# A batched matmul whose last store sends each partition's fourth row in 14 short transfers

## The chip, the cores and the metric

The kernel runs on one core of a Trainium2 chip. The metric is the device time of one execution in microseconds (us). Before the change it is 511.72 us, the median of 3 runs (511.66 to 512.26). A core has five engines that run side by side, PE (matmul), DVE (vector), ACT (scalar), POOL (GpSimd) and SP (which here only waits and issues transfers), and 16 transfer engines ("DMA engines" in the profile) that move data between the chip's main memory and the core's 128-partition memory.

## The reference

```python
def setup_inputs():
    batch, m, k, n = 32, 512, 1024, 768
    return {
        "x": np.random.randn(batch, m, k).astype(np.float32),
        "weight": np.random.randn(batch, k, n).astype(np.float32),
    }

def reference(x, weight):
    return np.matmul(x, weight).astype(np.float32)
```

32 independent products of a 512 x 1024 matrix with a 1024 x 768 matrix, all in float32 at the kernel's edges. The inputs are 64 MiB of x and 96 MiB of weight, the output is 48 MiB.

## The kernel before

The 32 batches are worked in 16 pairs. POOL loads x and weight and turns them into bfloat16 on the way (`load_x`, `load_w`); a pair of batches comes in one transfer of each, except at the edges of the program. PE transposes x (L173), DVE copies the transposed blocks out of PE's accumulator memory (L219, for the last pair L227), and PE multiplies (L165 and L138). ACT and DVE copy the results to `outs`, a buffer of four slots of one pair each (L261, L265, L270, L272).

Outputs of pairs 0 to 13 leave in one transfer for each pair, which POOL issues (`store`, L119). Pair 14 leaves in one transfer as well, issued by SP. The two batches of the last pair, 30 and 31, leave separately, each as soon as its own copies are done: `store_one` (L121 to L123), issued by SP. For these two, a partition holds four consecutive rows of the output, 4 x 768 float32 values, so that the store of one batch is 128 partitions x 3,072 values, 12,288 B of consecutive memory for each partition. `last_out(b)` is the place of batch b in `outs`, `one_view[b]` the place in the output.

SP's program (`on_sp`) first hands on the arrival of loads to PE in the order of the batches, then issues the three stores in a row: pair 14 (L379), batch 30 (L380), batch 31 (L381). Each of them waits for its own copies (`copied`), and counts its landing on the semaphore `s_fin`, 16 for a transfer. After that SP releases `s_zero` (L382), which POOL needs before it clears the semaphores. POOL's last step (`clear_on_pool`) is to wait until `s_fin` has reached 48, that is, until all three stores have landed (L392); after this the program ends.

Of the kernel before, what the change touches and what calls it, by code (L numbers as in the profile page):

```python
# [12 lines left out]
def kernel(  # L13
# [7 lines left out]
    B, M, K = x.shape  # L21
    _, _, N = weight.shape
# [5 lines left out]
    N2 = 2 * N  # L28
    ROW = MT * N
    PAIRS = B // 2  # L30
    HELD = 2
    GROUPS = 2 * MT
    W_SLOTS, X_SLOTS, OUT_SLOTS = 4, 2, 4

    pe, dve, act, pool, sp = nc.tensor, nc.vector, nc.scalar, nc.gpsimd, nc.sync
# [4 lines left out]
    one_view = out.rearrange("b (mi mo) n -> b mi (mo n)", mi=P)  # L40
# [20 lines left out]
    def sem(name):  # L61
        sems.append(nc.alloc_semaphore(name))
        return sems[-1]
# [7 lines left out]
    s_a, s_ap, s_d, s_dp = sem("s_a"), sem("s_ap"), sem("s_d"), sem("s_dp")  # L71
    s_st = [sem(f"s_st{i}") for i in range(OUT_SLOTS)]
    s_fin = sem("s_fin")


    def mm_done(b):
# [6 lines left out]
    def last_out(b):  # L83

        return outs[(PAIRS - 1) % OUT_SLOTS][:, ROW * (b % 2):ROW * (b % 2 + 1)]

# [3 lines left out]
    def together(b):  # L90
        return W_SLOTS <= b < B - 2

    def load_w(b):
        if together(b):
            if b % 2 == 0:
                pool.wait_ge(s_mm, mm_done(b + 1 - W_SLOTS))
                slots = all_ws[:, b // 2 % 2].rearrange("p r ko n -> p r (ko n)")
                pool.dma_start(out=slots, in_=w_two_view[b // 2]).then_inc(s_w[b % W_SLOTS], 16)  # L98
            return
        if b >= W_SLOTS:  # L100
            pool.wait_ge(s_mm, mm_done(b - W_SLOTS))
        pool.dma_start(out=ws[b % W_SLOTS], in_=w_view[b]).then_inc(s_w[b % W_SLOTS], 16)  # L102

    def loads_of_w(b):

        return sum(not (together(i) and i % 2) for i in range(b % W_SLOTS, b + 1, W_SLOTS))

    def load_x(k):
        if k >= X_SLOTS:
            pool.wait_ge(s_mm, mm_begun(k - X_SLOTS))  # L110
        pool.dma_start(out=xs[k % X_SLOTS], in_=x_view[k]).then_inc(s_x[k % X_SLOTS], 16)  # L111

    def copied(eng, j):
        eng.wait_ge(s_ap, j + 1)
        eng.wait_ge(s_dp, j + 1)

    def store(eng, a, sem):
        copied(eng, 4 * a + 3)
        eng.dma_start(out=two_view[a], in_=outs[a % OUT_SLOTS]).then_inc(sem, 16)  # L119

    def store_one(b):  # L121
        copied(sp, 2 * b + 1)
        sp.dma_start(out=one_view[b], in_=last_out(b)).then_inc(s_fin, 16)  # L123

# [49 lines left out]
    def take(s):  # L176
        pe.wait_ge(s, 1).then_inc(s, -1)  # L177
# [13 lines left out]
    def on_pe():  # L191
# [4 lines left out]
        pe.wait_ge(s_ident, 1)  # L196
        with nc.Fori(0, PAIRS, engines=[mybir.EngineType.PE], hint_back_edge=True):
            take(s_xr)
# [75 lines left out]
    def cast_first(eng, copy, rows):  # L274

        for mo in rows:
            if mo == MT - 1:
                eng.wait_ge(s_cast, 1)
                eng.wait_ge(s_rest, 16)
            last = copy(xs[0][:, mo], x_first[:, mo])  # L280
        return last

    def on_dve():
# [6 lines left out]
        cast_first(dve, dve.tensor_copy, range(MT // 2)).then_inc(s_cast, 1)  # L290
        turns = PAIRS // OUT_SLOTS

# [42 lines left out]
    def landed(eng, slot, n, ready, uses=1):  # L335

        eng.wait_ge(slot, 16 * n).then_inc(ready, uses)

    def on_pool():
# [17 lines left out]
        def stores(first, last):  # L357
            for a in range(max(first, 0), last):
                store(pool, a, s_st[a % OUT_SLOTS])


        for k in range(PAIRS - 2):
            load_x(k + 2)
# [3 lines left out]
            load_w(2 * k + 5)  # L367
        stores(PAIRS - 3 - HELD, PAIRS - 2)

    def on_sp():  # L370
        for b in range(B):
            if b == 0:
                sp.wait_ge(s_cast, 2).then_inc(s_xr, 1)
            elif b % 2 == 0:
                k = b // 2
                landed(sp, s_x[k % X_SLOTS], (k + 1) // X_SLOTS, s_xr)
            if not (together(b) and b % 2):
                landed(sp, s_w[b % W_SLOTS], loads_of_w(b), s_wr, 1 + together(b))
        store(sp, PAIRS - 2, s_fin)  # L379
        store_one(B - 2)  # L380
        store_one(B - 1)  # L381
        sp.sem_inc(s_zero, 1)  # L382

    def clear_on_pool():

        for i, s in enumerate(s_st):
            pool.wait_ge(s, 16 * len(range(i, PAIRS - 2, OUT_SLOTS)))
        pool.wait_ge(s_zero, 2)
        used = range(sems[0].num, s_fin.num)
        pool.dma_reset(used)  # L390
        pool.sem_clear(used)
        pool.wait_ge(s_fin, 48).then_inc(s_fin, -48)  # L392

    sp.dma_start(x_first, x_view[0, :, :MT])
    with tc.tile_critical(sync_engine=mybir.EngineType.Activation, no_gpsimd_drain=True):  # L395
        on_pool()
        tc.wait_critical_data_deps()
        on_pe()
        on_dve()
        on_act()  # L400
        on_sp()
        clear_on_pool()
# [30 lines left out]
```

## Time and profile before

| what | value |
|---|---|
| median of 3 runs | 511.72 us (511.66 to 512.26) |
| the profiled execution: span from first to last instruction | 509.6 us |
| bytes read from main memory, written | 167.77 MB, 50.33 MB |
| mean rate over the span | 428 GB/s |
| PE busy | 429.4 us, 84% |
| DVE, ACT, POOL busy | 211.7, 114.1 and 29.6 us |
| last store issued by SP | 498.43 us |
| from its issue to its landing | 10.2 us |

The profile comes from one execution of its own, whose span is 509.6 us; the runs' times cover a little more than the span. Lines such as "L123" are lines of the kernel. "SPq" is SP's issuing of transfers. In the rows of windows the columns are: the stretch in us from the span's start, its length, the busy time of PE, PE's weight loads, DVE, ACT and POOL (with the number of instructions), the clock granted to PE, the mean busy share of the 16 transfer engines, and the GB/s that they moved. A packet's bytes are put down to the window in which the packet starts, so in short windows a share can be above 1. In rows of transfers the last number is the us from the issue to the landing; in rows of one line's instructions the three numbers are the shortest, the median and the longest duration in ns, then the first and the last start in us.

### The profile page before, as it was taken

The numbers are of one execution on the slowest core, as the hardware profiler recorded it, in microseconds if no ns is written. First come the engines' busy times: TensorE is split into PE (matmuls) and PEld (weight loads), VectorE is DVE, ScalarE is ACT, GpSimd is POOL, SyncE is SP. The second block draws the span as 40 slices with busy tenths as digits, with TensorE's granted clock in tenths as the row PEclk, the third lists the DMA queues.
The fourth block names the chain that finished last, engine by engine and source line by source line (L and its number), as shares of the span: only waits on it lengthen the run. The fifth ranks groups of instructions, "written<-read, shape, count | busy, mean of one in ns | idle before, by whom it ended". The sixth has DMA issues, their size and how long they took to land. (4 is left out here: it accounts for less than half of the span.)

```text
span 509.6 us, 5832 instructions
## 1 busy us (share of the span) xinstructions
PE 429.4 (84%) x2560; PEld 172.8 (34%) x1536; DVE 211.7 (42%) x330; ACT 114.1 (22%) x195; POOL 29.6 (6%) x55
## 2 busy tenths in 40 slices
PE   0899989999899399993999949999399994999990
PEld 0525342443325034250343513434034341433420
DVE  1436362454635136351373514635146351454631
ACT  1131312223130231302313023230231302223230
POOL 3000000000101001010010100100001000100000
PEclk9999998999999799996999979999699997999996
DMA  8999999999999999999999999999999999999998
GB/s 262 216 211 216 225 207 221 215 305 247 221 212 230 432 234 214 217 237 432 226 215 217 247 433 216 218 217 259 420 217 217 219 267 408 218 215 229 432 430 347
DMA packets 9299, 135.29 MB, mean 266 GB/s; under 512 B 848, under 2 KB 848, under 8 KB 848
## 3 DMA queue, kind: packets, MB, share of 16 engines
q0 software_dynamic: 8720, 126.88, 96.8%
q1 hardware_dynamic: 576, 8.39, 4.0%
q14 instruction: 3, 0.02, 0.0%
HBM read 167.77 MB, written 50.33 MB: 428 GB/s over the span
## 5 line engine op out<-in xcount | busy, mean ns | idle before, releaser
L165 PE MATMUL pm<-w,xT 128*128 x1024 | 346.2, 389 | 42.0 <-DVE outs L270 38.7
L138 PE MATMUL pm<-w,xT 128*128 x1024 | 284.7, 278 | 0.0
L165 PEld LDWEIGHTS pm<-w,xT 128*128 128x128 bf16 x1024 | 102.3, 100 | 282.8 <-issue 241.0
L270 DVE COPY outs<-pm 64x512 f32<-64x512 f32 x128 | 88.2, 689 | 207.7 <-DVEq L268 206.3
L261 ACT COPY outs<-pm 64x512 f32<-64x512 f32 x128 | 74.2, 580 | 272.6 <-PE pm L138 168.4
L173 PE MATMUL pt<-ident,x 128*128 128x128 f32 x512 | 84.5, 307 | 24.8 <-PEq L177 14.5
L219 DVE COPY xT<-pt 128x1024 bf16<-128x1024 bf16 x120 | 77.7, 687 | 63.9 <-PE pt L173 63.6
L173 PEld LDWEIGHTS pt<-ident,x 128*128 128x128 f32 x512 | 71.2, 210 | 40.0 <-DVE xT L219 18.8
L265 ACT COPY outs<-pm 64x512 f32<-64x512 f32 x64 | 37.0, 579 | 99.5 <-PE pm L138 99.3
L272 DVE COPY outs<-pm 64x512 f32<-64x512 f32 x64 | 43.9, 686 | 0.0
L98 POOL DMA_DIRECT2D w<-in_weight_dram x13 | 9.2, 708 | 264.6 <-PE pm L138 264.6
L111 POOL DMA_DIRECT2D x<-in_x_dram x15 | 8.4, 557 | 123.2 <-PE pm L138 92.4
L119 POOL DMA_DIRECT2D out_dram<-outs x14 | 7.5, 539 | 7.1 <-DVE outs L272 7.1
L227 DVE COPY xT<-pt 128x512 bf16<-128x512 bf16 x16 | 5.7, 418 | 4.1 <-PE pt L173 4.1
L280 DVE CAST x<-outs 128x1024 bf16<-128x1024 f32 x2 | 1.3, 692 | 11.0 <-DMA outs<-in_x_dram 11.0
L102 POOL DMA_DIRECT2D w<-in_weight_dram x6 | 3.2, 544 | 26.5 <-PE pm L138 26.3
L280 ACT ACT_TABLE_LOAD x1 | 1.3, 1283 | 10.7 <-DMA outs<-in_x_dram 10.7
L280 ACT CAST x<-outs 128x1024 bf16<-128x1024 f32 x2 | 2.0, 1042 | 0.0
L340 POOL DMA_DIRECT2D x<-in_x_dram x1 | 0.7, 670 | 0.8 <-POOLq L417 0.8
L344 POOL TENSOR_SCALAR_AFFINE_SELECT ident<-ident 128x128 f32<-128x128 f32 x1 | 0.3, 284 | 0.2 <-POOL ident L342 0.2
L342 POOL MEMSET ident<- 128x128 f32 x1 | 0.2, 232 | 0.0
L417 POOL MEMSET const-float32-0.0<- 128x1 f32 x1 | 0.1, 99 | 0.2 <-issue 0.2
(3 smaller groups left out, 0.3 us busy)
## 6 DMA issues: line engine op xcount, KB each, us to landing
out_dram<-outs POOLq DMA_DIRECT2D x14, 3072.0 KB, 40.1
w<-in_weight_dram POOLq DMA_DIRECT2D x13, 3072.0 KB, 32.9
x<-in_x_dram POOLq DMA_DIRECT2D x15, 2048.0 KB, 34.3
w<-in_weight_dram POOLq DMA_DIRECT2D x6, 1536.0 KB, 30.5
out_dram<-outs SPq DMA_DIRECT2D x1, 3072.0 KB, 18.7
out_dram<-outs SPq DMA_DIRECT2D x2, 1536.0 KB, 13.6
outs<-in_x_dram SPq DMA_DIRECT2D x1, 2048.0 KB, 9.7
x<-in_x_dram POOLq DMA_DIRECT2D x1, 1024.0 KB, 11.6
```

What stands on the lines that cost most here:

```text
L98: pool.dma_start(out=slots, in_=w_two_view[b // 2]).then_inc(s_w[b % W_SLOTS], 16)
L111: pool.dma_start(out=xs[k % X_SLOTS], in_=x_view[k]).then_inc(s_x[k % X_SLOTS], 16)
L119: eng.dma_start(out=two_view[a], in_=outs[a % OUT_SLOTS]).then_inc(sem, 16)
L138: return pe.add_instruction(mybir.InstMatmult(name=nc.get_next_instruction_name(), engine=mybir.EngineType.PE, ins=[pe.lower_ap(moving), p ...
L165: last = pe.matmul(*args, start=(ko == 0), stop=(ko == KT - 1))
L173: last = pe.transpose(pts[g % 2][:, j, :], words[:, mo, j::JT], ident)
L219: return dve.tensor_copy(both[g // 2][:, :, :, g % 2].rearrange("p b j i r -> p j b i r"), pt)
L227: last = dve.tensor_copy(rows, pt[:, :, b])
L261: last = act.copy(*piece)
L265: act.copy(*pieces(b, p, 2)[0]).then_inc(s_ap, 1)
L270: last = dve.tensor_copy(*piece)
L272: dve.tensor_copy(*pieces(b, p, 2)[1]).then_inc(s_dp, 1)
```

## The change

Batch 30's store stays as it is. Batch 31's store is cut by columns: the first three of the four rows of each partition (2,304 values, 9,216 B) leave in one transfer over all 128 partitions, and the fourth row (768 values, 3,072 B) in 14 transfers over 15, 14, 13, 12, 11, 11, 10, 9, 8, 7, 6, 5, 4 and 3 partitions, which add up to 128. The 14 count on a semaphore of their own, `s_tail`, and POOL waits for it ahead of its last wait.

```diff
+    TAIL = (15, 14, 13, 12, 11, 11, 10, 9, 8, 7, 6, 5, 4, 3)
...
+    s_tail = sem("s_tail")
...
     def store_one(b):
         copied(sp, 2 * b + 1)
-        sp.dma_start(out=one_view[b], in_=last_out(b)).then_inc(s_fin, 16)
+        if b < B - 1:
+            sp.dma_start(out=one_view[b], in_=last_out(b)).then_inc(s_fin, 16)
+            return
+        most, at = ROW - N, 0
+        sp.dma_start(out=one_view[b, :, :most], in_=last_out(b)[:, :most]).then_inc(s_fin, 16)
+        for n in TAIL:
+            part = slice(at, at + n)
+            row = last_out(b)[part, most:]
+            sp.dma_start(out=one_view[b, part, most:], in_=row).then_inc(s_tail, 16)
+            at += n
...
         pool.dma_reset(used)
         pool.sem_clear(used)
+        ends = 16 * len(TAIL)
+        pool.wait_ge(s_tail, ends).then_inc(s_tail, -ends)
         pool.wait_ge(s_fin, 48).then_inc(s_fin, -48)
```

Only SP's program and the end of POOL's differ. SP's before, from the first load on (L394 the load, L119 the store of pair 14, L123 those of batches 30 and 31):

```order
L394 DMA outs<-in_x_dram 128x4096
L428 UNCONDITIONAL_BRANCH
L119 DMA out_dram<-outs 128x6144
L123 DMA out_dram<-outs 128x3072 x2
L395 UNCONDITIONAL_BRANCH
```

And SP's now, from the larger part of batch 31 on (L129), with the first rows of the 14 short transfers (L133):

```order
L129 DMA out_dram<-outs 128x2304
L133 DMA out_dram<-outs 15x768
L133 DMA out_dram<-outs 14x768
L133 DMA out_dram<-outs 13x768
L133 DMA out_dram<-outs 12x768
L133 DMA out_dram<-outs 11x768 x2
L133 DMA out_dram<-outs 10x768
L133 DMA out_dram<-outs 9x768
```

Where one issue stood for batch 31, 15 stand now, one after another on SP, with no wait between them.

## The prediction

> **What bounds the kernel now.** I read the page first (share of the transfer engines, the chain that ended last), then the windows of the last 12 us, then the rows of the store's own line.
>
> ```profile
> DMA  8999999999999999999999999999999999999998
> q1 hardware_dynamic: 576, 8.39, 4.0%
> 496.28 0.08 issue
> 496.36 0.68 DVE outs L270
> 497.04 0.71 DVEq L395
> 497.75 0.61 DVE outs L272
> 498.43 0.33 SPq L123 DMA_DIRECT2D out_dram<-outs  x1
> 498.50:506.50 8.00, 0.00 (x0) 0.00 (x0) 0.00 (x0) 0.00 (x0) 0.00 (x0) 0.58 1.00 429
> ```
>
> The transfer engines are at 0.9 or more in 38 of 40 slices, so transfers set the pace of the whole program. The chain of waits stops at the last copy on DVE, which ends at 498.36 us; 0.07 us later SP issues the last store. From there on no engine computes (every column of 498.50:506.50 is zero) and only stores move, at 429 GB/s. The span ends at 509.6, so the last 11.2 us are transfers and a closing. The change acts there alone.
>
> ```profile
> 505.94:506.40 0.46, 0.00 (x0) 0.00 (x0) 0.00 (x0) 0.00 (x0) 0.00 (x0) 0.50 1.00 427
> 506.40:506.80 0.40, 0.00 (x0) 0.00 (x0) 0.00 (x0) 0.00 (x0) 0.00 (x0) 0.50 1.15 492
> 506.80:507.30 0.50, 0.00 (x0) 0.00 (x0) 0.00 (x0) 0.00 (x0) 0.00 (x0) 0.50 0.58 246
> 507.30:507.70 0.40, 0.00 (x0) 0.00 (x0) 0.00 (x0) 0.00 (x0) 0.00 (x0) 0.50 0.30 123
> 507.70:508.10 0.40, 0.00 (x0) 0.00 (x0) 0.00 (x0) 0.00 (x0) 0.00 (x0) 0.50 0.08 31
> 508.10:508.60 0.50, 0.00 (x0) 0.00 (x0) 0.00 (x0) 0.00 (x0) 0.00 (x0) 0.50 0.00 0
> out_dram<-outs SPq DMA_DIRECT2D x1, 1536.0 KB, 10.2
> L392 POOLq EVENT_SEMAPHORE  x1: 17/17/17, 508.7 to 508.7; - x1
> ```
>
> These windows count the last packets; a packet's bytes stand in the window in which it starts. The last store is 128 rows of 12,288 B (1,536 KB), eight rows for each of 16 engines. At 427 GB/s an engine has 26.7 GB/s, so a row takes 0.46 us, and the first window is one full round: 427 x 0.46 us = 196 KB = 16 rows. The second is a full round too (492 x 0.40 = 197 KB). The third holds 246 x 0.50 = 123 KB, 10 rows; the fourth 49 KB, 4 rows; the fifth 12.4 KB, one row; the sixth none. So the engines don't end together: 16-10 = 6 end around 507.05, 10-4 = 6 around 507.5, 4-1 = 3 around 507.9, and one around 508.35. Issued at 498.43 and landed 10.2 us later, the store is down at 508.6; POOL's last wait (L392) ends at 508.7, and the rest, 0.9 us, is the program's end.
>
> The mean of those ends is (6 x 507.05 + 6 x 507.5 + 3 x 507.9 + 508.35) / 16 = 507.46. Spreading the same bytes so that all engines end together would save 508.35 - 507.46 = 0.9 us, 0.17% of 511.72. **That is the most that any redistribution of this store can gain.**
>
> **The change, part by part.** The 128 rows of the last store become 128 rows of 9,216 B in one transfer and 128 rows of 3,072 B in 14.
>
> *Bytes per engine.* If row j of a short transfer runs on engine j, engine e gets as many tail rows as there are transfers longer than e: 14, 14, 14, 13, 12, 11, 10, 9, 8, 7, 6, 4, 3, 2, 1, 0 for engines 0 to 15 (sum 128), against 8 quarter rows each now. A quarter row takes 3,072 B / 26.7 GB/s = 0.115 us. So engine 0 moves 6 x 0.115 = 0.69 us more, engine 5 0.35 more, engine 8 the same, engine 11 0.46 less, engine 15 0.92 less. No row of this trace shows a transfer of fewer than 128 rows, so the assignment is the first unknown. The Trainium skill, page "DMA: Bandwidth & Descriptors", section "Why a DMA increments its semaphore by 16 and not by 1", states that a transfer issued from SP with n of at most 16 rows uses n engines, the lowest-numbered ones; by that rule the staircase is as above, and no run so far shows it.
>
> *Packets.* The page has 576 packets on q1 for SP's four transfers, 144 each: one for each of 128 rows and 16 small ones that close the transfer. The tail adds 128 row packets and up to 128 closing ones; engine 0 gets 14 of each for the 8 quarter rows that were part of larger packets.
>
> ```profile
> 490.00:498.00 8.00, 6.16 (x38) 1.76 (x18) 3.62 (x6) 2.32 (x4) 0.00 (x0) 1.00 1.02 436
> 503.20:503.65 0.45, 0.00 (x0) 0.00 (x0) 0.00 (x0) 0.00 (x0) 0.00 (x0) 0.50 1.03 437
> 503.65:504.10 0.45, 0.00 (x0) 0.00 (x0) 0.00 (x0) 0.00 (x0) 0.00 (x0) 0.50 1.03 437
> ```
>
> With 24,576 B rows among the packets the rate is 436 GB/s, with 12,288 B rows alone 429: 1.6% of 0.46 us, so a packet costs at most about 0.007 us beyond its bytes. Some 22 extra packets on engine 0 are then 0.15 us: lower bound 0, upper bound in the rival below. I take 0.14, and engine 0's net change is +0.83 us.
>
> *Issue on SP.* 14 more issues.
>
> ```profile
> L123 SPq DMA_DIRECT2D out_dram<-outs x2: 332/332/333, 488.0 to 498.4; - x2
> L394 SPq DMA_DIRECT2D outs<-in_x_dram x1: 377/377/377, 0.7 to 0.7; - x1
> 1.50:2.00 0.50, 0.00 (x0) 0.00 (x0) 0.00 (x0) 0.00 (x0) 0.50 (x2) 1.00 1.58 328
> ```
>
> An issue of 128 rows takes 0.33 to 0.38 us. Short ones lie between nothing and that; I take the upper end, 0.37 with the step between two. SP then ends at 498.8 + 14 x 0.37 = 504.0, and with the 1.0 us that the first load needs from its issue (0.7) to its first bytes (after 1.5) the last tail row is ready at 505.0. The cover is the backlog. An engine that ends at 506.9 today starts its own eight rows 8 x 0.457 = 3.65 us earlier, and has sent the 9,216 B parts by 506.9 - 8 x 0.115 = 506.0. So the issues cost **0**. Without that cover they would cost up to 5.2 us. What SP does after them (L382 releases POOL's clearing) waits for nothing on the path: POOL clears long before 508.7.
>
> *The added wait on POOL.* It precedes the last one; nothing is queued behind it but the end. If the tail is last, one more wait runs after it: 0.02 us busy (L392), 0.1 with its step. I take +0.06.
>
> *Sum.* Here the second unknown enters: which engines are the late ones. The windows don't name them. Lower bound (best order, ends rising with the number): engine 0 ends at 506.9 + 0.83 = 507.73, engine 5 at 507.2 + 0.46 (0.35 and packets) = 507.66, engine 6 at 507.4 + 0.34 = 507.74, engine 11 at 507.6 - 0.41 = 507.2, engine 15 at 508.35 - 0.9 = 507.45. The last is 507.75 instead of 508.35, a gain of 0.55 to 0.6; less 0.06, **-0.5 us**. Upper bound (the latest engine among the first three): 508.35 + 0.83, +0.9 us with the wait. The first load went out in one issue of 0.377 us. If an issue serves the engines one after another, the first engine starts ahead of the last, and rows that split evenly over 16 engines leave it ahead. That argues, without showing it, for ends that rise with the number, and I choose the lower end. The profiled execution would go from 509.6 to 509.1. The median of the runs, 511.72, lies 2.1 us above that span; I keep that difference: **511.2**.
>
> **Rivals.**
>
> *Late engines at other numbers* (a chance of 0.30). A late engine with a low number gets more work. If one of the three that end at 507.9 has 13 or 14 tail rows, it ends at 508.65 to 508.73: +0.4 with the wait, 512.1; if the last one is among the first three, 512.6. For it: the steps of the ends (6, 6, 3, 1 per round) are whole rows, not a slope in the number. Against: nothing in the trace. An assignment that gives every engine about 8 rows also belongs here: only packets and the wait are left, +0.1, 511.8. The Trainium skill, same page, section "Latency and other measured facts", says that transfer engines 7 and 15 are usually slower than the rest. Worked out here: engine 15 at 508.35 - 0.9, and engine 7, with 9 rows, at about 508.0 + 0.21 = 508.2, so -0.1 and 511.6; the trace neither shows nor denies it, and I give it 0.10 of the 0.30.
>
> *Closings that stand in line* (0.14), the case on the slower side. Each of 14 transfers on engine 0 must be confirmed before its count rises. Today the last packet starts after 507.7, ends at about 508.35, and the landing is at 508.6: about 0.3 us. If an engine holds its next row until that is done, engine 0 needs 14 x (0.115 + 0.3) = 5.8 us after 506.0 and ends at 511.8: +3.5 us, 515.2. It decides from 0.17 us per transfer, (508.35 - 506.0) / 14. Against it: from 506.9 - 3.65 = 503.25 on, the store of batch 30 hands over to the last one, each engine closes one transfer, and 503.20:504.10 stays at 437 GB/s; a hold of 0.3 us on 16 engines would take a third out of a 0.9 us window. For it: there a closing comes once in 3.65 us, in the tail every 0.12. The Trainium skill, same page, section "Rules for kernel authors", says to coalesce small transfers since those under 64 KB are mostly overhead; these are 45 to 9 KB. The unbroken rate at the handover speaks against a cost in sequence.
>
> *Issues too slow* (0.05). Engine 0 needs the fourteenth transfer by 507.6. That allows (507.6 - 1.0 - 498.8) / 14 = 0.56 us for each. At 0.75 the last row would be ready at 510.3: +2.1 us, 513.8. All three issues measured are at 0.38 or less.
>
> **How the numbers follow.** Forecast 0.51: 511.2, with its own range 510.9 to 511.5. Rivals 0.30, 0.14 and 0.05. 0.2% is 1.02 us, about what a measurement of this kernel can tell from no change. The gain is capped at 0.9 us, so faster than 510.7 needs a kinder run as well: 0.10. Slower than 512.74: both waiting rivals (0.19) and a little of the late engines: 0.21. The rest, 0.69, is within 0.2%. The range 510.8 to 512.8 holds the forecast and nearly all of the first rival, and leaves out the two rivals of 2 us and more.
>
> **What would show it.** In the changed profile: 14 issues at the tail's line of 0.38 us or less, ending by about 504; 429 GB/s until 506; then a steeper fall, with no packet starting after about 507.7, and the last wait of POOL at 508.1 to 508.2. If rows still start after 508, the late engines are among those with many tail rows. If the windows after 506 show a long, thin stretch of under 60 GB/s (one to three engines at work), closings or issues stand in line. The forecast is wrong if the last landing doesn't move to before 508.5.

## The result, and the profile after

The changed kernel takes 513.43 us (median of 7 runs, 513.20 to 513.96), the kernel before 511.91 us in the same session (7 runs, 511.39 to 512.26). The ratio is 1.003, with a 95% interval of 1.0021 to 1.0039: 1.5 us slower. The profiled execution's span grew from 509.6 to 511.4 us.

The first rows are those of the last stores' lines in the changed kernel, the larger part of batch 31 (L129), the 14 short transfers (L133), and POOL's two last waits (L404 for the short ones, L405 for the large ones). The numbers are the shortest, median and longest duration in ns, then the first and the last start in us. Two words are used from here on: a *closing* is the small packet of 4 B with which an engine ends its share of a transfer, and a *landing* is the step of the transfer's semaphore that comes of it.

```profile
L129 SPq DMA_DIRECT2D out_dram<-outs x1: 332/332/332, 498.5 to 498.5; - x1
L133 SPq DMA_DIRECT2D out_dram<-outs x14: 272/322/1819, 498.9 to 508.8; - x14
L404 POOLq EVENT_SEMAPHORE  x1: 17/17/17, 510.4 to 510.4; - x1
L405 POOLq EVENT_SEMAPHORE  x1: 17/17/17, 510.5 to 510.5; - x1
```

The second are the windows of the same stretch as in the prediction.

```profile
498.50:505.90 7.40, 0.00 (x0) 0.00 (x0) 0.00 (x0) 0.00 (x0) 0.00 (x0) 0.62 0.99 424
505.90:506.40 0.50, 0.00 (x0) 0.00 (x0) 0.00 (x0) 0.00 (x0) 0.00 (x0) 0.50 0.96 393
506.40:506.80 0.40, 0.00 (x0) 0.00 (x0) 0.00 (x0) 0.00 (x0) 0.00 (x0) 0.50 0.78 300
506.80:507.30 0.50, 0.00 (x0) 0.00 (x0) 0.00 (x0) 0.00 (x0) 0.00 (x0) 0.50 0.82 252
507.30:507.70 0.40, 0.00 (x0) 0.00 (x0) 0.00 (x0) 0.00 (x0) 0.00 (x0) 0.50 0.29 92
507.70:508.10 0.40, 0.00 (x0) 0.00 (x0) 0.00 (x0) 0.00 (x0) 0.00 (x0) 0.50 0.44 123
508.10:508.60 0.50, 0.00 (x0) 0.00 (x0) 0.00 (x0) 0.00 (x0) 0.00 (x0) 0.50 0.23 80
508.60:509.60 1.00, 0.00 (x0) 0.00 (x0) 0.00 (x0) 0.00 (x0) 0.00 (x0) 0.50 0.21 52
509.60:510.10 0.50, 0.00 (x0) 0.00 (x0) 0.00 (x0) 0.00 (x0) 0.00 (x0) 0.50 0.03 6
510.10:511.40 1.30, 0.00 (x0) 0.00 (x0) 0.00 (x0) 0.00 (x0) 0.00 (x0) 0.50 0.00 0
```

Up to 505.9 nothing differs (424 GB/s, 425 before). Then the rate falls, and instead of ending at 508 it runs out in a thin stretch to 510: 52 GB/s between 508.6 and 509.6 is what two of 16 engines move. POOL is released at 510.4, before the change at 508.7, and passes one wait more. The last tail row starts at 509.71.

SP's issues did not take 0.37 us each. They begin at 498.9, and the last one ends at 508.8 + 0.27 = 509.1. One by one, from the trace (us from the span's start, and how long each took):

```
498.87 1.82   500.74 1.54   502.32 0.96   503.32 0.96   504.33 1.60
505.97 0.35   506.36 0.33   506.73 0.32   507.09 0.30   507.43 0.30
507.76 0.30   508.10 0.30   508.45 0.30   508.78 0.27
```

The first five took 1.0 to 1.8 us, the other nine 0.27 to 0.35. The two transfers over 11 rows are numbers 5 and 6, with 1.60 and 0.35, so it isn't the number of rows.

### The profile page after: what moved, and what is told of

Read it like the earlier page. It is cut to its first block, busy times and chain, and to the rows that moved or that the text cites. A ratio compares the mean times of both kernels' runs of the same rounds, so it can differ in the third digit from the quotient of the medians.

```text
span 511.4 us, 5847 instructions
## 1 busy us (share of the span) xinstructions
PE 430.3 (84%) x2560; PEld 173.1 (34%) x1536; DVE 211.6 (41%) x330; ACT 113.9 (22%) x195; POOL 29.5 (6%) x55
```

## The experiments

### Where the short transfers are issued, and how they are cut

**The same 14, issued by ACT.** ACT waits for the last copies and issues them in its own queue.

```diff
+        store_tail(act, B - 1)
+        act.sem_inc(s_zero, 1)
...
-        pool.wait_ge(s_zero, 2)
+        pool.wait_ge(s_zero, 3)
```

> The 14 short transfers are issued by ACT, in its own queue, once all copies of batch 31 are done; all else as in the change. Theory 'full queue' (SP's issue of a short transfer waits until its queue has room for it on each engine that it uses; the rows of batches 30 and 31 fill it): ACT's queue is empty, so the first 7 or 8 issues take 0.30 to 0.37 us each, later ones may wait, the last is issued before 506, and the engines never run dry: 511.2 to 512.3, at least 1.0 below the change. Theory 'short transfers' (an issue of fewer than 16 rows is slow in itself, as the change's first five with 1.0 to 1.8 us): again 10 us of issues, 513.0 to 513.8. Theory 'late engines' (the order of issue is harmless, the staircase loads engines that are late anyway): issues fast, and still 512.8 or more.

513.97 us, ratio 1.0041 (1.0027 to 1.0055) to the kernel before. ACT's issues (L137):

```profile
L137 ACTq DMA_DIRECT2D out_dram<-outs x14: 293/525/1972, 498.6 to 509.4; - x14
```

An empty queue of its own changes nothing: again up to 1.97 us, again done only at 509.6. The theory that SP's own queue had no room falls. In the trace the first short row starts at 502.5, though its issue ended at 499.2, and only then does the rest trickle in.

**One tail transfer over 128 partitions.**

```diff
-    TAIL = (15, 14, 13, 12, 11, 11, 10, 9, 8, 7, 6, 5, 4, 3)
+    TAIL = (128,)
```

> The fourth rows leave in one transfer over 128 partitions, issued by SP right behind the three others: the cut by columns without the staircase and without short transfers. 'Full queue': this one issue waits some us (to about 503 to 505) until each engine has room for 8 rows and a closing, but then all rows are there before the engines need them: 511.8 to 512.2. 'Short transfers': issued in 0.33 us, 511.8 to 512.2. If the smaller rows themselves are slow, 512.5 or more.

511.90 us, ratio 1.0002 (0.9993 to 1.0011): no loss.

```profile
L133 SPq DMA_DIRECT2D out_dram<-outs x1: 1767/1767/1767, 499.0 to 499.0; - x1
```

The issue took 1.77 us, about as long as the first of the 14 (1.82), though it covers 128 rows and all 16 engines. Cutting by columns is harmless, and one slow issue is hidden by the backlog, as predicted.

**Whole rows, over 112, 12 and 4 partitions.**

```diff
-    TAIL = (15, 14, 13, 12, 11, 11, 10, 9, 8, 7, 6, 5, 4, 3)
+    TAIL = (12, 4)
...
-        most, at = ROW - N, 0
-        sp.dma_start(out=one_view[b, :, :most], in_=last_out(b)[:, :most]).then_inc(s_fin, 16)
+        at = P - sum(TAIL)
+        sp.dma_start(out=one_view[b, :at], in_=last_out(b)[:at]).then_inc(s_fin, 16)
```

> No cut by columns: 112 partitions leave whole, then 12, then 4, so that the lowest-numbered four engines get 9 rows of 12,288 B, the next eight 8 and the last four 7. 'Full queue': two short transfers add only four packets to the fullest engine, issues wait 1 to 2 us at most, all done by 503. The time then tells the order of the engines alone: 511.4 to 511.6 if the last four engines are the late ones, 511.9 to 512.4 if the late ones are among the others, since the first four are then 0.46 later. 'Short transfers': the same, since two issues of 1.8 us stay hidden.

511.95 us as a median of 11, ratio 1.002 (1.0005 to 1.0035). The gain of 0.3 to 0.5 us that late last four engines would have brought is excluded, and the other branch agrees: the late ones are among the others. Seven of the 11 runs lie between 511.5 and 512.0, the other four between 513.0 and 515.0, and what made those longer isn't shown. So the two issues, of 0.96 and 1.18 us, cost at most little: the median is 0.2 us above that of the kernel before (511.77).

**Eight transfers over 16 partitions.** No staircase: each engine moves what it moves in the kernel before.

```diff
-    TAIL = (15, 14, 13, 12, 11, 11, 10, 9, 8, 7, 6, 5, 4, 3)
+    TAIL = (16,) * 8
```

> The fourth rows leave in eight transfers over 16 partitions each, issued by SP: as many short transfers as batch 31 needs, but no staircase, and every engine moves the bytes it moves in the kernel before. 'Full queue': the first four or five issues take 1.0 to 1.8 us each as in the change, the last is issued at 506.5 to 507.5, 511.9 to 512.6. 'Short transfers' (if it is the count under 16 that is slow): all eight at 0.30 to 0.37 us, issued by 502, 511.8 to 512.1. 'Late engines': 511.8 to 512.1, since the staircase is gone.

512.65 us, ratio 1.0015 (1.0006 to 1.0024). The issues and the windows of the end:

```profile
L133 SPq DMA_DIRECT2D out_dram<-outs x8: 420/1028/1495, 499.3 to 506.8; - x8
508.20:509.30 1.10, 0.00 (x0) 0.00 (x0) 0.00 (x0) 0.00 (x0) 0.00 (x0) 0.50 0.00 0
L404 POOLq EVENT_SEMAPHORE  x1: 17/17/17, 509.3 to 509.3; - x1
```

Five slow issues here too, with 16 rows each: a count under 16 isn't the cause. All the same, this kernel loses 0.9 us (512.65 against 511.77) without a staircase, and the windows show where: the last row starts before 508.2, and POOL is released only at 509.3. The last closing starts at 508.28 by the trace's packet records and counts on the semaphore 0.95 us later; in the kernel before that time is 0.35 us (508.29, then 508.65). The last five landings stand 0.186 us apart: closings have begun to queue.

**Half the staircase in seven issues.**

```diff
-    TAIL = (15, 14, 13, 12, 11, 11, 10, 9, 8, 7, 6, 5, 4, 3)
+    TAIL = (64, 15, 13, 11, 9, 8, 8)
```

> The fourth rows of 64 partitions leave in one transfer, those of the other 64 in transfers over 15, 13, 11, 9, 8 and 8 partitions: half the staircase in 7 issues instead of 14. If the time of the issues is what was lost, SP is done by 506.8 to 507.4, about 2 us earlier than in the change, and the last landing falls to 508.6 to 509.2: 511.8 to 512.4. If the loss is the staircase on late engines or the closings one after another, about half of the change's 1.5 to 1.7 us stays: 512.5 to 512.7.

512.65 us, ratio 1.0013 (1.0004 to 1.0022) and so within the second answer (512.5 to 512.7), closings or late engines. Its profiled execution is one of the longer ones (span 511.2; the others 510.3 to 511.1) and shows the end at its clearest:

```profile
L133 SPq DMA_DIRECT2D out_dram<-outs x7: 295/1097/1805, 499.5 to 506.8; - x7
508.20:509.20 1.00, 0.00 (x0) 0.00 (x0) 0.00 (x0) 0.00 (x0) 0.00 (x0) 0.50 0.09 34
509.20:510.20 1.00, 0.00 (x0) 0.00 (x0) 0.00 (x0) 0.00 (x0) 0.00 (x0) 0.50 0.01 3
L404 POOLq EVENT_SEMAPHORE  x1: 17/17/17, 510.2 to 510.2; - x1
```

SP is done at 507.1, and POOL waits until 510.2. The last six steps of the short transfers' semaphore come at 509.26, 509.45, 509.64, 509.82, 510.01 and 510.20, one every 0.19 us: what one engine's closings look like when they queue. So the issues alone don't make the loss.

### How long a closing takes, and which engines are late

**Markers over 112, 12 and 4 partitions.** The last 512 B of each partition leave in three transfers with a semaphore each, behind the rest.

```diff
-    TAIL = (15, 14, 13, 12, 11, 11, 10, 9, 8, 7, 6, 5, 4, 3)
+    TAIL = (112, 12, 4)
...
-        most, at = ROW - N, 0
+        most, at = ROW - 128, 0
```

> The last store sends 11,776 B of each partition in one transfer, the last 512 B in transfers over 112, 12 and 4 partitions, each counted on its own semaphore. The three short ones queue on each engine behind the large one, so the landings tell when groups of engines end: 4 landings for the lowest-numbered four, 12 for the lowest twelve, 16 for all. Theory 'late engines low' (the staircase of the change met late engines among those with many rows): the latest of the 4 or of the 12 lands within 0.2 us of the latest of all. Theory 'ends rise with the number' (as predicted): the 4 land first, all before 507.8, and the latest of the 16 is none of the 12. Time 511.7 to 512.3 either way.

512.32 us, ratio 1.001 (1.0001 to 1.002). Landings of the 4: 507.69, 507.81, 508.31 and 508.72. The latest of the 12: 509.21, of the 16: 509.02; the middle of the 16 is 507.6. So the latest engine is among the first twelve, and two of the first four are among the latest three. This is the theory "late engines low", by its condition on the 12; for the 4 the difference to the latest is 0.5 and not 0.2.

**Markers over 112, 10, 3, 2 and 1 partitions,** otherwise the same.

> As the markers, with the last 512 B of each partition in transfers over 112, 10, 3, 2 and 1 partitions, each on its own semaphore: the 1 tells when the first engine ends, the 2 the second, the 3 the third. 'Late engines low', and the same ones in every run: the latest of the 3 lands 0.4 us or more after the middle of the 16, and the latest of all is among the 10. If the late engines change from run to run: none of the first three is late. Time 511.8 to 512.8.

512.30 us in one run. The issues, then the landings of the single markers from the trace's semaphore events:

```profile
500.05 5.27 SPq L133 DMA_DIRECT2D out_dram<-outs  x5
```

```
over 112: 507.31 ... 507.92 508.37 508.43 509.02 509.13
over  10: 507.51 507.52 507.58 507.61 507.67 507.75 507.80 508.09 508.54 509.20
over   3: 507.755 508.261 508.711
over   2: 507.929 508.881
over   1: 508.113
```

Each engine's landings can be followed down the columns: the first one's at 507.58, 507.755, 507.929 and 508.113; the second's at 508.54, 508.711 and 508.881; the third's at 508.09 and 508.261. **Each step is 0.17 to 0.18 us.** All five issues were over at 505.3, two us earlier, and a 512 B row with its closing occupies the engine for only 0.03 us in the packet records. So on one engine a transfer's landing is reported 0.17 us or more after the one before it, even where the bytes are next to none. Late engines: the second (1.0 us behind the first), the third, one of the fourth to tenth, which is the latest of all, and one above the tenth. In the kernel with markers over 12 and 4 the second, the third and one of the fifth to the twelfth were late too. Lateness isn't ordered by number; why these engines are late isn't shown.

**The whole staircase with rows of 512 B.**

```diff
-        most, at = ROW - N, 0
+        most, at = ROW - 128, 0
```

> The change with short rows of 512 B instead of 3,072 B: the same 15 issues, the same closings, but the staircase moves only a sixth of the bytes. If the issues set the end (the last one ends at 509.1 and its rows land 1.3 later), nothing changes: 513.0 to 513.5. If the bytes on late engines set it, a late engine ends 14 x 0.1 us earlier than in the change, and the issues are not in the way: 512.0 to 512.5.

514.26 us, ratio 1.0045 (1.0029 to 1.0062): slower than the change, though the staircase moves a sixth of the bytes. The windows of the end:

```profile
L133 SPq DMA_DIRECT2D out_dram<-outs x14: 272/322/1701, 499.4 to 508.9; - x14
509.20:509.80 0.60, 0.00 (x0) 0.00 (x0) 0.00 (x0) 0.00 (x0) 0.00 (x0) 0.50 0.03 6
509.80:511.10 1.30, 0.00 (x0) 0.00 (x0) 0.00 (x0) 0.00 (x0) 0.00 (x0) 0.50 0.00 0
L404 POOLq EVENT_SEMAPHORE  x1: 17/17/17, 511.1 to 511.1; - x1
```

The last closing starts at 509.77, after it no packet does, and POOL is released 1.35 us later. The large transfer's last landing is at 508.88, the tail's at 511.12: 2.24 us. In the trace a line of twelve landings, 0.18 to 0.19 us apart, leads from the one to the other. In the change the same difference is 510.40 - 508.13 = 2.27 us, with rows six times as large. Moving fewer bytes in the tail only makes the large part later: (3,072 - 512) B x 8 rows / 26.7 GB/s = 0.77 us, and 513.43 + 0.77 = 514.2 is what was measured. Neither expectation named that sum; "the issues set the end" gave the nearer one.

### Why an issue takes more than a microsecond

**Ten short loads halfway** (batch 16), while POOL's loads fill the engines.

```diff
+    PROBE = (15, 14, 13, 12, 11, 11, 10, 9, 8, 7)
...
+            if b == B // 2:
+                for i, n in enumerate(PROBE):
+                    here = scratch[:n, 192 * i:192 * (i + 1)]
+                    sp.dma_start(out=here, in_=x[0, :n, :192]).then_inc(s_probe, 16)
```

> The kernel before, and halfway (when the loads of batch 16 have arrived) SP issues ten short loads of 15, 14, 13, 12, 11, 11, 10, 9, 8 and 7 rows of 768 B into a buffer that nobody uses. At that time no transfer of SP or ACT is waiting, while POOL's transfers keep all 16 engines busy. Theory 'shared room' (each engine takes about 16 waiting packets of SP's and ACT's transfers together, an issue waits for room): the first seven or so issues take 0.30 to 0.37 us each, only then do they slow down. Theory 'slow hand-over' (what SP and ACT issue is handed to the engines one transfer after another, and while the engines are busy each takes 1 to 2 us, however few its rows): from the second or third on every issue takes 0.9 us or more, ten of them 8 to 18 us. The total time is not compared; it should stay within 511 to 516.

**Ten short stores halfway,** from `ident` into rows of the last batch that are written anew later.

```diff
+                    there = out[B - 1, :n, 64 * i:64 * (i + 1)]
+                    sp.dma_start(out=there, in_=ident[:n, :64]).then_inc(s_probe, 16)
```

> The probe halfway again, with ten short stores in place of the ten short loads: 15, 14, 13, 12, 11, 11, 10, 9, 8 and 7 rows of 256 B from the identity matrix into rows of the last batch, which that batch's own store writes anew at the end, after a wait for the probe. The engines are full of POOL's loads of x and weight at that time. If short stores are slow to issue by their direction: 1 to 2 us each as at the end of the change. If it is the company (engines full of stores): 0.29 to 0.41 us each as the short loads. For the closings: if each transfer on one engine is confirmed only after the one before it, landings of one engine follow at 0.17 us or more; beside loads each packet waits longer anyway. The total time is not compared; 511 to 516.

The two probes took 511.72 and 512.19 us, one run each, and only their traces are used.

**The three large stores on POOL,** the 14 short ones on SP, so that nothing large of SP waits.

```diff
-        store(sp, PAIRS - 2, s_fin)
-        store_one(B - 2)
-        store_one(B - 1)
+        store_tail(B - 1)
```

> The three large stores (pair 14, batch 30, the three rows of batch 31) are issued by POOL, the 14 short ones by SP as in the change, so that nothing large of SP or ACT is waiting while the engines stay as full of stores. POOL clears the semaphores only after the large ones. Theory 'large ones ahead' (an issue of SP or ACT is slow while large transfers of SP or ACT still wait at the engines): all 14 at 0.29 to 0.37 us, done by 504. Theory 'short stores' (short stores are slow beside full engines): 1 to 2 us each as in the change. The time, if the issues are fast: with 'late engines low' (a late engine with 11 to 14 tail rows at 0.124 us each, a row with its closing) the loss stays, 512.6 to 513.2; if the issues were the whole loss, 511.6 to 512.3.

The issues and the engines' load meanwhile, first of the probe of loads, then of the probe of stores, then of the kernel with the large stores on POOL:

```profile
L385 SPq DMA_DIRECT2D scratch<-in_x_dram x10: 295/338/409, 258.1 to 261.6; - x10
258.10:261.90 3.80, 3.59 (x24) 1.40 (x14) 3.24 (x5) 0.49 (x1) 0.23 (x1) 1.00 0.97 207
```

```profile
L386 SPq DMA_DIRECT2D out_dram<-ident x10: 297/338/418, 258.3 to 261.8; - x10
```

```profile
L135 SPq DMA_DIRECT2D out_dram<-outs x14: 274/530/1516, 499.0 to 509.5; - x14
498.90:505.10 6.20, 0.00 (x0) 0.00 (x0) 0.00 (x1) 0.00 (x0) 0.53 (x1) 0.66 0.97 410
```

Ten short ones in a row take 0.30 to 0.42 us each beside full engines, loads and stores alike. "Slow hand-over" falls, and so does "short stores are slow by their direction". With the large stores on POOL the late issues are slow again (up to 1.52 us, 513.84 us, ratio 1.0039 with 1.0024 to 1.0053), so "large ones of SP ahead" falls too. Left is the company: beside engines full of loads (207 GB/s) an issue takes 0.3 to 0.4 us, beside engines full of stores (410 to 424 GB/s) mostly 0.9 to 2.0 us from the second in a row on, and 0.3 again when the stores run out. That it is the stores follows by elimination only; how they would do it wasn't found.

**The 14 on POOL.**

```diff
+        store_tail(pool, B - 1)
...
+        pool.wait_ge(s_tail, 16 * len(TAIL))
         pool.wait_ge(s_zero, 2)
```

> The 14 short transfers are issued by POOL after its last store, and POOL clears the semaphores only when they have landed (0.3 us more at the end). POOL has been filling the engines' own other queue all along at 0.54 us an issue. 'Slow hand-over' as a stage that only SP and ACT share: 14 issues at 0.5 to 0.6 us, done by 506.5, before the engines run dry; rows may be spread over the engines in another way; 511.8 to 512.9. If any short transfer is slow beside full engines, whoever issues it: issues of 1 us and more, 513.2 or more.

513.96 us, ratio 1.004 (1.0024 to 1.0055).

```profile
L137 POOL DMA_DIRECT2D out_dram<-outs x14: 497/497/516, 500.8 to 507.2; - x14
```

POOL isn't held up: 0.50 us for each, done at 507.7. The tail still landed only at 511.2, 3.5 us after its last issue; its semaphore took 224 steps, 14 closings on each of the 16 engines, where SP's took 128 closings. The last nine landings of the tail stand 0.17 to 0.18 us apart, up to the last one at 511.16. In this execution the larger part of batch 31 was issued 1.8 us later than in the change (500.24 against 498.48), for a reason that isn't known, and POOL's clearing lies behind the landing, so the total isn't compared. What is shown is that closings queue at the end also where no issue is late.

## Why the prediction was wrong

The forecast was 511.2 and the range ended at 512.8; it is 513.43. What the prediction said of the place held: the transfers of the last 11 us, nothing before, a cut by columns without cost, 0.1 us for the added wait. One of its signs of trouble came as well, a stretch of under 60 GB/s after 506. Three steps failed.

**"A packet costs at most about 0.007 us beyond its bytes"**, and with it 0.14 us for 22 packets. As the price of sending, this held: in the change's packet records twelve tail rows with their closings follow each other on one engine 0.12 us apart. What the sum put at nothing is the time from one landing to the next. Measured by the single markers, landings on one engine follow at 0.17 to 0.18 us, in the change and its variants at 0.18 to 0.20. That is more than a 3,072 B row takes (0.115), so on a busy engine the landings fall behind the rows. This is the rival "closings that stand in line", given 0.14, and it was half right. Closings do stand in line, but the rows don't wait for them: the rival took 0.3 us from packet to landing on top of each row, 5.8 us in all, while in truth the rows go on and the landings are 0.17 to 0.20 apart. Its own threshold, 0.17 us per transfer, is where the measured value lies. The evidence held against it, an unbroken rate at the handover from batch 30 to 31, was no evidence: closings come once in 3.65 us there, and packets go on starting while closings wait: the staircase of 512 B rows had sent all packets 1.35 us before its last landing. The Trainium skill, page "DMA: Bandwidth & Descriptors", section "Rules for kernel authors", warns that transfers under 64 KB are mostly overhead, and here that agrees: 9 to 45 KB, with 0.17 us of closing for each row's 0.115.

**"Ends rise with the number"**, chosen as the lower bound. The markers put the second engine 1.0 us behind the first and the latest of all between the fourth and the tenth. The change's own trace leads to the same place. From the last landing of the large part twelve landings of the tail run on in one line, to the last one of all (us from the span's start):

```
large part: 508.130
tail:       508.331 508.525 508.713 508.901 509.090 509.278
            509.465 509.651 509.837 510.023 510.209 510.395
```

In the packet records twelve tail rows follow the last row of the large part without a gap, until 509.13. The records carry no engine numbers, so this line is followed by its spacing and its count. In the prediction's staircase one engine has 12 tail rows, the fifth. So the latest engine got four rows more than its eight, where the prediction had the latest ones lose rows. This is the first rival, given 0.30, though neither with one of the first four engines, which it priced, nor with engine 7 or 15, which have 9 and no tail rows.

The line also divides the loss. The engine's rows are all sent 0.83 us after the last row of the kernel before ends (509.13 against 508.30); four rows more are 0.5 of that, and the rest isn't explained. From there to the last landing it takes 1.27 us where the kernel before needs 0.35: 0.92 us for closings in line. Together that is the 1.75 us by which the last landing comes later (510.40 against 508.65).

**"So the issues cost 0."** They took 10.2 us, not 5.2, since the duration came from issues with nothing issued just ahead, and the first five took 1.0 to 1.8 us beside the stores. The last one ended at 509.06, and the last row starts 0.65 us after that. With the 14 on ACT, and with the large stores on POOL, such a last row takes 0.52 to 0.55 us from its start to its landing. By these numbers the late issues alone would put the change's last landing at an estimated 510.25. The rival "issues too slow" (0.05) needed 0.56 us for each; the mean was 0.73.

So in the change two limits end within 0.15 us of each other: closings on the latest engine (510.40) and the supply of short transfers (510.25, estimated). How long it is from the start of the last closing, on whatever engine, to the last landing tells in which runs closings stood in line at the very end (trace, us from the span's start):

```
                         last closing starts   last landing   between
before                         508.29             508.65        0.35
one tail transfer              508.30             508.77        0.48
the 14 on ACT                  510.51             510.84        0.33
large stores on POOL           510.67             511.01        0.33
the change                     509.92             510.40        0.48
half the staircase             509.32             510.20        0.88
eight over 16                  508.28             509.23        0.95
the 14 on POOL                 510.07             511.16        1.09
staircase of 512 B rows        509.77             511.12        1.35
```

With the 14 on ACT and with the large stores on POOL the last landing comes as soon after its closing as in the kernel before, and no line of landings stands at the end: there the late supply put down the last row. Where the supply is early or the rows are short, the closings rule. In the change they rule by a little, as the line of landings above shows. The runs show that curing the supply isn't enough (seven issues over by 507.1 still landed at 510.2, eight over by 507.2 still lost 0.9 us), and if the estimate of 510.25 is right, curing the closings alone would not be enough either. A kernel with slow issues and few closings wasn't tried, so the share of the issues by themselves isn't measured. Nothing of the cap on the gain, 0.9 us for perfect balance, was reached: two short transfers of whole rows brought nothing either (1.0005 to 1.0035), and none of these versions beats the single store.

## What to carry to other kernels

Count transfers by engine, not only bytes: here each closing in line on an engine cost 0.17 to 0.19 us, so at the end of a program, where nothing covers it, a transfer that moves less than an estimated 4.5 to 5 KB on an engine (0.17 to 0.19 us at 26.7 GB/s) costs more than its bytes. Before evening out the ends of the engines, find out with markers of their own semaphore which engines are late; a mean over 16 engines, as in the windows, gives the size of the unevenness and not its order. And take the duration of an issue from a place with the same load: 0.33 us from a lone issue was wrong by a factor of three to five and a half for the second to the sixth in a row beside engines full of stores.

## What I had not expected of the hardware

- The time from the start of the last closing to the last landing is no constant: 0.35 us after one large store, up to 1.35 us after many short ones, with no packet of the store on any engine in that time.
- A short transfer can start long after its issue, in an empty queue. With SP's large transfer just issued, ACT's first short row started 3.3 us after its issue had ended, in a queue of its own that was empty. In the probe halfway SP's first short row also started only 3.4 us after its issue's end (258.5 to 261.95), with nothing of SP or ACT ahead of it and POOL's packets on all engines; with the large stores on POOL it is 3.4 us again. So it isn't shown that SP and ACT hold each other up.
- The semaphore of the 14 short transfers took 142 steps: 128 closings, one for each row and so for each engine that a transfer uses, and one more with each issue's end. The Trainium skill, page "DMA: Bandwidth & Descriptors", section "Why a DMA increments its semaphore by 16 and not by 1", says that a transfer over n rows, here at most 15, uses n engines and that the issuer writes the rest of the 16 at once; the count and the times of those 14 steps (0.12 to 0.17 us after the end of each of the slow issues) agree. That these are always the same, lowest-numbered ones fits the markers, whose single landings continue the columns of the wider ones, and the twelve landings of the latest engine.
